# Two-layer encoder trunk on one core: the order of the first FFN's start, the norms behind the mixers, the first mixer's attention gaps and one weight split of the second mixer are changed

## The chip, the cores and the metric

The kernel runs on one NeuronCore of a Trainium2 chip. The metric is device time in microseconds from launch to end; a lower time is better. The core has five engines that run side by side, each through its own list of instructions in order: TensorE (PE, matmuls), VectorE (DVE), ScalarE (ACT), GpSimd (POOL) and SyncE (SP, which only issues transfers). They wait for each other through semaphores.

## The reference

Two groups of tokens (512 and 256, model width 1024) go through the same two layers. Everything is float32.

```python
def swiglu(h, wg, wu, wd):
    return (jax.nn.silu(h @ wg) * (h @ wu)) @ wd          # 1024 -> 2816 -> 1024

def even_layer(x, ...):
    x = x + 0.5 * swiglu(rmsnorm(x, f1_n), f1_g, f1_u, f1_d)
    x = x + mixer_ab(rmsnorm(x, mix_n), ...)   # gated MLP | windowed attention (8 heads, 2 kv heads)
    x = x + 0.5 * swiglu(rmsnorm(x, f2_n), f2_g, f2_u, f2_d)

def odd_layer(x, ...):
    x = x + 0.5 * swiglu(...)
    x = x + mixer_c(rmsnorm(x, mix_n), ...)    # 2-D neighbourhood attention, 16 heads, then @ w_out
    x = x + 0.5 * swiglu(...)

y = rmsnorm(odd_layer(even_layer(x)), final_norm)
```

## The kernel before

The 768 tokens are one block of columns. An activation tile holds 128 features on the partitions and up to 768 tokens; work goes by halves of 384 tokens. A float32 product is made of three passes over halves of the operands: `wsplit` (L113) cuts a weight block of 128x512 into a rounded high part `whi` (cast on ACT, L125) and the rest `wlo` (a subtraction on DVE or POOL, L126). `split` (L221) does the same with activations (names ending in h and l, L224 and L225). A product needs high x high, high x low and low x high.

The six stages are FFN, first mixer, FFN, FFN, second mixer, FFN, with a norm between them. The FFNs take the 2816 hidden columns in 11 pairs of blocks and use seven products per 2x2 step instead of eight. The products are called b11, b21, t2, t3, n4, t1 and b22 in the order of use, each for the gate and then for the up weights; each is 12 matmuls of 384 columns for gate and 12 for up. Weight sums (`s`, L817) and activation sums (`tmp`, L439) feed some of them. The first four pairs are early pairs: their b11 and b21 are computed while the norm of the tokens isn't known yet, so the norm's factors come in later. Four matmuls with a diagonal matrix (`diag`, L326 and L324, against `onesr`) spread the factors of the tokens over the partitions, two for each half of the tokens.

The behaviour that the change touches:

- **Start.** `tok_norm` (L275) squares six token blocks for each half on ACT (L289) and takes the mean's power -0.5 on POOL (`rsqrt`, L337). `rest` (L441) makes the operands t3, n4, t1 and b22 on ACT and DVE. `hidden` (L625) takes gate and up to the gated hidden value: two products with the norm's factors (L631, L633), silu on ACT (L632) and the product sg·v (L634, `scalar_tensor_tensor`). `settle` (L723) runs the last five products of an early pair, and `parts` (L586) makes a weight operand one product ahead.
- **Norm behind a mixer.** `norm_half` (L358) calls `norm_tok` (L256). Without `power`, `rsqrt` computes the reciprocal root on DVE by Newton steps on 128x3 tiles (L341 to L350).
- **First mixer's attention.** `attention` (L1349) is a generator beside the projections. In each of twelve rounds it traces a `score` (L1291), the `values` (L1328) of the round before, and the `turn` (L1315): a transpose of the probabilities `p` by matmuls with the identity (`ident`). The yields between them are delays in modelled PE time, so they set how many projection matmuls stand between; the gap is 5.2 us in the model.
- **Output product of the second mixer.** `mixer_out` (L1050) is used by both mixers; `begun` is set in the first one only. `rows(m)` (L1095) loads and splits the weights of output block m. In the second mixer `ready` (L1066) traces the splits of the attention's output ahead of `rows(0)`. `oh` and `ol` are the halves of the attention's output `o`, six blocks for each half of the tokens.

PE's order is the order of the trace, steered by these delays. The orders of DVE, ACT, POOL and SP are set by a scheduler by priorities; `high_priority` moves work forward, and `issue_after(x)` keeps an instruction behind x. POOL also issues some weight transfers (L108).

Of the kernel before, what the change touches and what calls it, by code (L numbers as in the profile page):

```python
# [9 lines left out]
F32 = mybir.dt.float32  # L10
# [4 lines left out]
ALU = mybir.AluOpType  # L15

P = 128
# [38 lines left out]
class Trunk:  # L56
# [4 lines left out]
    def __init__(self, ctx, tc, aps, phases=PHASES):  # L61
        self.tc, self.nc, self.aps, self.phases = tc, tc.nc, aps, phases
        self.units = []
        self.woff = self.pi = 0
        self.t = 0.0
        self.chains = []
        self.spare = []
        self.first = []
        self.copied = []
        self.ps1 = []  # L70
        self.exps = []
        self.hids = []
        self.tok = []
        pool = lambda name, bufs, **kw: ctx.enter_context(tc.tile_pool(name=name, bufs=bufs, **kw))
        self.cp = pool("const", 1)
        self.xp = pool("x", 1)
        self.rawp = pool("raw", 4)
        self.wp = pool("w", NW)
        self.np_ = pool("norm", 1)
        self.sp = pool("small", 1, side="right")  # L80
        self.mm = pool("mm", 4, space=bass.MemoryType.PSUM)
        self.aux = pool("aux", 4, space=bass.MemoryType.PSUM)
        self.dram = pool("spill", 1, space=bass.MemoryType.DRAM)
        self.guards = {}
        self.side = "left"
# [29 lines left out]
    def wsplit(self, src, eng=None, keep=False):  # L115

        nc = self.nc
        self.pi += 1
        if keep:
            hi, lo = (self.fw.tile([P, 512], F32R, tag="s", name=f"k{n}{self.pi}", bufs=8) for n in ("hi", "lo"))  # L120
        else:
            hi = self.wp.tile([P, 512], F32R, tag="whi", name=f"whi{self.pi}")
            lo = self.wp.tile([P, 512], F32R, tag="wlo", name=f"wlo{self.pi}")
        hi, lo = (t.rearrange("p (a b) -> p a b", a=src.shape[1]) for t in (hi, lo))
        self.cast = nc.scalar.copy(hi, src).ins  # L125
        (eng or nc.gpsimd).tensor_tensor(out=lo, in0=src, in1=hi.bitcast(F32), op=ALU.subtract)  # L126
        return hi, lo

    def unit(self, name, k0, nk, c0, n):
# [145 lines left out]
    def tok_norm(self, h):  # L275

        nc = self.nc
        while len(self.copied) < TOKW[h]:
            yield 0.2
        sm = self.sp.tile([P, 3, 6], F32, tag="sm", name="sm", bufs=3)  # L280
        it = self.sp.tile([P, 6], I32, tag="smi", name="smi", bufs=2)
        a, y, b = (sm[:, i, :3] for i in range(3))
        for i in range(6):
            if h:
                with self.tc.issue_after(self.loading):
                    self.tok_load()
            t = self.tok[6 * h + i]
            with self.tc.issue_after(self.copied[-1]) if h else nullcontext():
                nc.scalar.activation(t, t, AF.Square, accum_out=(b if i % 2 else a)[:, i // 2 : i // 2 + 1])  # L289
        with self.tc.high_priority() if h == 0 else nullcontext():  # L290
            nc.vector.tensor_tensor(out=a, in0=a, in1=b, op=ALU.add)
            self.rsqrt(y, a, 1.0 / D, a, b, it[:, :3], True)
            self.early[h] = self.diags(y)
        self.spawn(self.norm_rt(h, DELAYT[h]))
# [63 lines left out]
    def norm_half(self, h, d0=1.8, d1=4.0):  # L358

        c0, c1 = HALVES[h]  # L360
        yield d0
        if not self.tok:
            with self.tc.high_priority():
                y = self.norm_tok(self.acc, c0, c1)
        yield d1
        with self.tc.high_priority():
            self.r[h] = self.spread(self.early[h]) if self.tok else self.norm_spread(y)
# [73 lines left out]
    def rest(self, *after):  # L441

        (a0, a1), (c0, c1) = HALVES
        yield STEPS[0]
        fresh = bool(self.tok)
        while fresh and (len(self.copied) < 6 or not self.early):
            yield 0.2
        self.holds = [self.copied[5], self.rooted] if fresh else list(after)
        for n in ("t3", "n4", "t1", "b22"):
            while fresh and n == "b22" and len(self.copied) < 2 * EARLY:  # L450
                yield 0.2
            for k in range(4):
                with ExitStack() as stack:
                    for ins in self.holds + ([self.copied[2 * EARLY - 1]] if fresh and n == "b22" else []):
                        stack.enter_context(self.tc.issue_after(ins))
                    if fresh and n == "t3":
                        stack.enter_context(self.tc.high_priority(offset=500))
                    if n == "t1":
                        self.gain_split(n, k, self.tmp[k], k, self.ngains)
                    elif n == "t3":  # L460
                        t = self.etile("tmp")
                        self.combine(t, self.x[k][:, c0:c1], -1, k, self.tmp[k + 4])
                        self.split(*self.b[n][k], t)
                    elif n == "n4":
                        t = self.tmp["t2", k]
                        self.combine(t, self.x[k + 4][:, a0:a1], 0, k + 4, t)
                        self.split(*self.b[n][k], t)
                    else:
                        self.split(*self.b[n][k], self.tmp[k + 4])
                yield STEPS[1]  # L470
            self.made += [n]

# [42 lines left out]
    def ffn(self, pre):  # L515
# [49 lines left out]
        def pair(p):  # L565
# [9 lines left out]
                        a[n, i + 1, 1], a[n, i + 1, 2] = r[:, 0:4, :], r[:, 4:8, :]  # L575

            h = hs[p] = {}
            s, bank, e = {}, {}, {}
            steps = iter(())

            def sums(n, name):
# [4 lines left out]
            def parts(n, b):  # L586
                name = {"t2": "s2", "t3": "s3", "t1": "s1", "b22": "s4"}.get(b)
                soon = fresh and not p and b == "t3"
                with self.tc.high_priority(offset=500 if soon else None) if b == "t2" and p in urgent or soon else nullcontext():
                    return self.wsplit(sums(n, name) if name else a[n, 2, 2], nc.vector)  # L590

            def product(n, w, b, key, start, st=None):
# [29 lines left out]
                nc.vector.tensor_tensor(out=t, in0=bank[key, n], in1=t, op=ALU.add)  # L622
                next(steps, None)

            def hidden(i, half, g, u):  # L625

                self.run_until(lambda: half in scales)
                h[i, half] = t = g if half else etile("sg")
                v = u if half else etile("v")
                r = rt[:, HALVES[half][0] : HALVES[half][1]]  # L630
                nc.vector.tensor_tensor(out=t, in0=g, in1=r, op=ALU.mult)  # L631
                nc.scalar.activation(t, t, AF.Silu, scale=-1.0 if i else 1.0)  # L632
                self.freed = nc.vector.tensor_tensor(out=v, in0=u, in1=r, op=ALU.mult).ins  # L633
                nc.vector.scalar_tensor_tensor(out=t, in0=t, scalar=-0.5 if i else 0.5, in1=v, op0=ALU.mult, op1=ALU.mult)  # L634

            def begin(n, p1):

# [76 lines left out]
            def entry(ahead=False):  # L714
                if not loaded:
                    settled()
                    loaded.append(True)
                if ahead:
                    return None
                with self.tc.issue_after(self.hids[1]) if fresh and not p else nullcontext():  # L720
                    return parts("gate", "t2")

            def settle(st):  # L723

# [2 lines left out]
                for i, (n, b) in enumerate(todo):  # L727
# [14 lines left out]
                    if n == "up":  # L742
                        if b == "t3":
                            fourth()
                        if b == "n4":
                            hidden(1, 0, bank["Y", "gate"], bank["Y", "up"])
                        elif b == "t1":
                            hidden(1, 1, e["gate", "u3"], e["up", "u3"])
                        elif b == "b22":
                            hidden(0, 1, e["gate", "u2"], e["up", "u2"])  # L750

            if early:
# [4 lines left out]
                p2()  # L757
                yield
                with self.tc.high_priority():
                    hidden(0, 0, bank["X", "gate"], bank["X", "up"])  # L760
                self.hids.append(self.freed)
                yield
            if early:
# [6 lines left out]
            if early:  # L770
                if p + 1 < EARLY - 1:
                    addeds[p + 1](behind + 3 if fresh and p == 0 else None)
                settle(now)
            else:
                for f in (p1, p6, p2, p7, p4, p5, p3) if p == NPAIR - 1 else (p1, p6, p2, p7, p5, p3, p4):
                    f()
# [273 lines left out]
    def mixer_out(self, name, ot, chain, cols=False, begun=None):  # L1050
# [44 lines left out]
        def rows(m):  # L1095
# [1 line left out]
                loaded[4] = self.raw(name, 0, 4, m * P, 2 * P)  # L1097
                loaded[2] = self.unit(name, 4, 2, m * P, 2 * P)
            c = m % 2 * P
            hi, lo = self.wsplit(loaded[4][:, :, c : c + P], self.nc.vector if begun and m < 3 else None)  # L1100
            return [(hi[:, k, :], lo[:, k, :]) for k in range(4)] + [tuple(t[:, c : c + P] for t in k) for k in loaded[2]]

        def first(m, h, w):
# [106 lines left out]
    def mixer0(self):  # L1210
# [138 lines left out]
        def attention(gap):  # L1349
            cur = None  # L1350
            for kv in (0, 1):
                for n in range(6):
# [5 lines left out]
                    if cur:  # L1358
                        values(*cur[:3], tt)
                        valued.append(cur[:2])  # L1360
                    yield gap
                    cur = new
                    tt = turn(*cur)
                    yield 0.3 * gap
            yield 1.0
            values(*cur[:3], tt)

# [555 lines left out]
```

## Time and profile before

| | us |
|---|---|
| three runs | 2575.41, 2578.79, 2583.24 |
| median | 2578.79 |
| profiled execution | 2577.02 |
| its span, first to last instruction | 2575.3 |
| PE, DVE, ACT, POOL busy | 2548.0, 2204.1, 1365.4, 225.3 |

The profile is of one execution. A page gives busy times, the span in 40 slices, the chain of work that ended last and the costliest groups. Beside it the trace answers questions on a stretch: a timeline row gives start, duration, engine, line, output<-input, shapes, and in brackets the idle time of the engine ahead of it and what ended it. Matmuls are pipelined, so a matmul's duration overlaps the next one's; distances between their starts are what counts. Where a matmul waits, its pipeline refills too, so that PE loses somewhat more than the idle time in brackets. A row of slices gives the time, PE's busy time and number of matmuls, the granted clock of PE (1.00 is full speed), the DMA engines' share and GB/s.

### The profile page before, as it was taken

The page shows a single profiled execution, that of the slowest core. Times are in us where ns is not written, and L with a number is a line of the kernel's source. Part 1 is how long each engine was busy: PE and PEld are TensorE (multiplying, and loading weights), DVE is VectorE, ACT ScalarE, POOL GpSimd, SP SyncE. Part 2 cuts the span into 40 slices and gives each one's busy share as a digit, 9 for nine tenths or more (in the row PEclk, how much of TensorE's full clock was granted, in tenths as well). Part 3 has the DMA queues.
Part 4 walks back from the last instruction along what each step waited for, and adds up shares of the span by engine and source line. Part 5 has one row for each costly group of instructions (what it writes and reads, how often), then busy time and mean ns, then how long its engine had stood idle before and what let it go on. Part 6 is the DMA issues. An engine that isn't in the chain of part 4 may idle for free.

```text
span 2575.3 us, 41296 instructions
## 1 busy us (share of the span) xinstructions
PE 2548.0 (99%) x15114; PEld 2487.0 (97%) x15114; DVE 2204.1 (86%) x4558; ACT 1365.4 (53%) x2869; POOL 225.3 (9%) x355
## 2 busy tenths in 40 slices
PE   9999999999999999999999999999999999999998
PEld 8999999988899999999999999999899999999997
DVE  7988898888889889889998889986777699888897
ACT  7544454556666545445654445454545475454543
POOL 2100000000031320000100000002222221000000
PEclk9999999999999999999999999999999999999999
DMA  8422221421236432222542222242221354222222
GB/s 266 111 82 66 79 70 66 147 78 54 66 120 159 126 120 69 73 78 81 149 98 82 69 80 66 66 146 64 64 64 41 108 151 103 87 76 68 74 67 74
DMA packets 84029, 238.68 MB, mean 93 GB/s; under 512 B 10481, under 2 KB 19505, under 8 KB 83825
## 3 DMA queue, kind: packets, MB, share of 16 engines
q1 hardware_dynamic: 69136, 204.93, 24.3%
q0 software_dynamic: 14400, 30.81, 6.0%
q8 instruction: 119, 1.95, 0.3%
q14 instruction: 86, 0.70, 0.1%
q10 hardware_dynamic: 288, 0.29, 0.0%
HBM read 226.56 MB, written 15.07 MB: 94 GB/s over the span
## 4 chain that ended last, share of the span: by engine, by line
PE 89%; DVE 7%; ACT 2%; issue 1%; DMA 1%; POOL 0%; SPq 0%; DVEq 0%; ACTq 0%; POOLq 0%
PE ps_mm L155 54%; PE ps_aux L155 33%; DVE wlo L126 1%; PE ps_aux L159 1%; DMA raw<-in_w 1%; ACT p L1195 1%; DVE p L1189 1%; DVE p L1205 0%; DVE tmp L439 0%; DVE tl L225 0%; DMA tok<-in_xt 0%; ACT whi L125 0%; DVE sg L634 0%; DVE s L817 0%; DVE o L1341 0%
## 5 line engine op out<-in xcount | busy, mean ns | idle before, releaser
L125 ACT CAST whi<-s 128x512 fp32r<-128x512 f32 x496 | 304.4, 620 | 398.4 <-DVE s L817 118.1
L125 ACT CAST whi<-raw 128x512 fp32r<-128x512 f32 x472 | 286.8, 618 | 222.5 <-PE ps_mm L155 85.4
L126 DVE TENSOR_TENSOR wlo<-s,whi 128x512 fp32r<-128x512 f32 x496 | 337.4, 686 | 67.6 <-ACT whi L125 61.2
L126 DVE TENSOR_TENSOR wlo<-raw,whi 128x512 fp32r<-128x512 f32 x439 | 300.8, 692 | 19.0 <-ACT whi L125 15.5
L155 PE MATMUL ps_mm<-db,whi 128*128 128x384 f32 x864 | 219.2, 334 | 0.0
L155 PE MATMUL ps_aux<-dt,whi 128*128 128x384 f32 x864 | 219.2, 334 | 0.0
L155 PEld LDWEIGHTS ps_aux<-dt,whi 128*128 128x128 f32 x864 | 156.0, 188 | 0.0
L155 PEld LDWEIGHTS ps_mm<-db,whi 128*128 128x128 f32 x864 | 156.0, 188 | 0.0
L155 PE MATMUL ps_mm<-xh,whi 128*128 128x512 f32 (+1 forms) x416 | 145.0, 349 | 0.0
L155 PE MATMUL ps_aux<-dt,wlo 128*128 128x384 f32 x432 | 144.3, 334 | 0.0
L155 PE MATMUL ps_mm<-db,wlo 128*128 128x384 f32 x432 | 144.3, 334 | 0.0
L155 PE MATMUL ps_mm<-xl,whi 128*128 128x512 f32 (+1 forms) x416 | 140.2, 337 | 0.0
L155 PE MATMUL ps_mm<-xh,wlo 128*128 128x512 f32 (+1 forms) x416 | 140.2, 337 | 0.0
L108 POOL DMA_DIRECT2D s<-in_w x96 | 75.0, 858 | 693.2 <-PE ps_aux L155 306.8
L622 DVE TENSOR_TENSOR u<-ps_aux,u 128x384 f32<-128x384 f32 x176 | 97.2, 552 | 9.5 <-PE ps_aux L155 9.4
L155 PE MATMUL ps_aux<-dh,whi 128*128 128x384 f32 x384 | 97.5, 334 | 0.0
L1195 ACT ACTIVATE p<-p,st 128x256 f32<-128x256 f32 (+3 forms) x144 | 68.9, 480 | 52.8 <-DVE st L1193 52.7
L873 DVE TENSOR_TENSOR x<-ps_aux,x 128x384 f32<-128x384 f32 x160 | 85.1, 552 | 12.0 <-PE ps_aux L155 11.9
L873 DVE TENSOR_TENSOR x<-ps_mm,x 128x384 f32<-128x384 f32 x160 | 86.5, 552 | 5.3 <-PE ps_mm L155 5.0
L155 PEld LDWEIGHTS ps_mm<-xh,whi 128*128 128x128 f32 x416 | 78.9, 190 | 9.0 <-issue 0.7
L155 PEld LDWEIGHTS ps_mm<-xh,wlo 128*128 128x128 f32 x416 | 78.8, 189 | 8.6
L617 ACT COPY u<-ps_mm 128x384 f32<-128x384 f32 x176 | 83.2, 473 | 6.7 <-PE ps_mm L155 6.6
(520 smaller groups left out, 8187.6 us busy)
## 6 DMA issues: line engine op xcount, KB each, us to landing
raw<-in_w SPq DMA_DIRECT2D x282, 512.0 KB, 3.6
s<-in_w POOLq DMA_DIRECT2D x96, 256.0 KB, 4.3
row<-in_w SPq DMA_DIRECT2D x32, 512.0 KB, 3.7
row<-in_w SPq DMA_DIRECT2D x32, 256.0 KB, 3.9
xdm<-x SPq DMA_DIRECT2D x16, 384.0 KB, 2.4
x<-in_x SPq DMA_DIRECT2D x16, 192.0 KB, 4.7
tok<-in_xt SPq DMA_DIRECT2D x12, 256.0 KB, 6.1
xold<-xdm SPq DMA_DIRECT2D x8, 384.0 KB, 3.0
```

The source lines that it names most:

```text
L108: ins = (eng or self.nc.sync).dma_start(raw, src, **kw).ins
L125: self.cast = nc.scalar.copy(hi, src).ins
L126: (eng or nc.gpsimd).tensor_tensor(out=lo, in0=src, in1=hi.bitcast(F32), op=ALU.subtract)
L155: self.nc.tensor.matmul(out, lhsT=lhsT, rhs=rhs, start=start, stop=stop, **kw)
L159: self.nc.tensor.transpose(out, src, self.ident)
L617: nc.scalar.copy(e[n, out], bank[key, n])
L622: nc.vector.tensor_tensor(out=t, in0=bank[key, n], in1=t, op=ALU.add)
L873: nc.vector.tensor_tensor(out=o, in0=ps, in1=o, op=ALU.add)
L1189: nc.vector.tensor_tensor_reduce(out=outs[i], in0=ps_list[i], in1=adds[i], scale=1.0, scalar=init[i], op0=ALU.add, op1=ALU.max, accum_out= ...
L1195: ins = nc.scalar.activation(outs[i], outs[i], AF.Exp, bias=nm[:, i : i + 1], accum_out=sm[:, i : i + 1])
```

## The change

It has five parts. (1) In the first FFN: the token squares of the second half wait for operand t3 and, the last two, for the cast of pair 0's first t2 weights; the loads of their tokens are traced at once; some weight sums are kept behind a first low half (`self.lower`), the b22 sums behind the n4 operands. (2) In early pairs, the product sg·v of two `hidden` calls, (0, 0) and (1, 0), is put off to the end of `settle`, and in pair 0 the whole call (1, 1). (3) `norm_half` passes `self.mixed` as `power`: both mixers' norms take the power on POOL. (4) In `mixer_out` the low half of block 0's weights is made on DVE in the second mixer as well, where before POOL made all of them (L1100); the first mixer's blocks 0 to 2 stay on DVE. (5) In `attention` the delays are 0.8 and 0.5 of the gap instead of 1.0 and 0.3.

```diff
-        (eng or nc.gpsimd).tensor_tensor(out=lo, in0=src, in1=hi.bitcast(F32), op=ALU.subtract)
+        low = (eng or nc.gpsimd).tensor_tensor(out=lo, in0=src, in1=hi.bitcast(F32), op=ALU.subtract).ins
+        if eng is nc.vector and not self.marked:
+            self.lower = low
...
+        for _ in range(6 * h):
+            with self.tc.issue_after(self.loading):
+                self.tok_load()
         for i in range(6):
-            if h:
-                with self.tc.issue_after(self.loading):
-                    self.tok_load()
             t = self.tok[6 * h + i]
-            with self.tc.issue_after(self.copied[-1]) if h else nullcontext():
+            while h and (len(self.thirds) < 3 or i >= 4 and not self.marked):
+                yield 0.2
+            with self.tc.issue_after(self.marked if i >= 4 else self.thirds[2]) if h else nullcontext():
...
-                y = self.norm_tok(self.acc, c0, c1)
+                y = self.norm_tok(self.acc, c0, c1, self.mixed)
...
+                    if fresh and n == "n4":
+                        self.negated = self.halved
+                    elif fresh and n == "t3":
+                        self.thirds.append(self.halved)
...
-                with self.tc.high_priority(offset=500 if soon else None) if b == "t2" and p in urgent or soon else nullcontext():
+                with ExitStack() as stack:
+                    if b == "t2" and p in urgent or soon:
+                        stack.enter_context(self.tc.high_priority(offset=500 if soon else None))
+                    if fresh and not p and b == "b22":
+                        stack.enter_context(self.tc.issue_after(self.negated))
+                    if soon or fresh and not p and (n, b) == ("up", "t2"):
+                        stack.enter_context(self.tc.issue_after(self.lower))
...
                         if b == "n4":
-                            hidden(1, 0, bank["Y", "gate"], bank["Y", "up"])
+                            put_off.append(hidden(1, 0, bank["Y", "gate"], bank["Y", "up"], True))
+                        elif b == "t1" and p:
+                            hidden(1, 1, e["gate", "u3"], e["up", "u3"])
                         elif b == "t1":
-                            hidden(1, 1, e["gate", "u3"], e["up", "u3"])
+                            put_off.append(lambda: hidden(1, 1, e["gate", "u3"], e["up", "u3"]))
...
-                    hidden(0, 0, bank["X", "gate"], bank["X", "up"])
+                    put_off.append(hidden(0, 0, bank["X", "gate"], bank["X", "up"], True))
...
                 settle(now)
+                for f in put_off:
+                    f()
...
-            hi, lo = self.wsplit(loaded[4][:, :, c : c + P], self.nc.vector if begun and m < 3 else None)
+            hi, lo = self.wsplit(loaded[4][:, :, c : c + P], self.nc.vector if m < (3 if begun else 1) else None)
...
-                    yield gap
+                    yield 0.8 * gap
                     cur = new
                     tt = turn(*cur)
-                    yield 0.3 * gap
+                    yield 0.5 * gap
```

The orders of both kernels show what moved. Lines of the changed kernel are some 4 to 30 higher than those of before.

DVE in the start of the first FFN, before, from the weight sum ahead of the t3 operands on (`sg`, `v`: of hidden; `s`: weight sums; `t3xl`: low halves of t3; `wlo`: low halves of weights):

```order
L817 TENSOR_TENSOR s_686<-s_584,row 128x512
L225 TENSOR_TENSOR t31l<-tmp,t31h 128x384
L225 TENSOR_TENSOR t32l<-tmp,t32h 128x384
L631 TENSOR_TENSOR sg<-ps_mm_526,acc 128x384
L817 TENSOR_TENSOR s_700<-s_588,row 128x512
L817 TENSOR_TENSOR s_726<-row 128x512
L126 TENSOR_TENSOR wlo_689<-s_686,whi_688 128x512
L633 TENSOR_TENSOR v<-ps_mm_561,acc 128x384
```

and the same place of the changed kernel:

```order
L647 TENSOR_TENSOR sg<-ps_mm_524,acc 128x384
L229 TENSOR_TENSOR t31l<-tmp,t31h 128x384
L229 TENSOR_TENSOR t32l<-tmp,t32h 128x384
L847 TENSOR_TENSOR s_661<-s_582,row 128x512
L649 TENSOR_TENSOR v<-ps_mm_559,acc 128x384
L445 SCALAR_TENSOR_TENSOR tmp<-x_107,ngains,tmp 128x384
L128 TENSOR_TENSOR wlo_664<-s_661,whi_663 128x512
L445 SCALAR_TENSOR_TENSOR tmp<-x_108,ngains,tmp 128x384
```

The two weight sums s_700 and s_726 no longer stand between the first sum and its `wlo`; the first sum itself stands behind t32l. Later on DVE, at the end of pair 0's products, the changed kernel has this (u: products kept in SBUF, s_948: weight sum for pair 1's t2 of up):

```order
L638 TENSOR_TENSOR u_745<-ps_aux_871,u_745 128x384
L652 SCALAR_TENSOR_TENSOR u_768<-u_768,u_789 128x384
L649 TENSOR_TENSOR u_745<-u_745,acc 128x384
L847 TENSOR_TENSOR s_948<-s_671,row 128x512
L652 SCALAR_TENSOR_TENSOR u_720<-u_720,u_745 128x384
L847 TENSOR_TENSOR s_974<-row 128x512
L128 TENSOR_TENSOR wlo_951<-s_948,whi_950 128x512
```

where before the like sum s_951 stood ahead of the add u_749 that waits for PE:

```order
L225 TENSOR_TENSOR b223l<-tmp,b223h 128x384
L817 TENSOR_TENSOR s_922<-s_692,row 128x512
L622 TENSOR_TENSOR u_724<-ps_aux_852,u_724 128x384
L817 TENSOR_TENSOR s_951<-s_696,row 128x512
L126 TENSOR_TENSOR wlo_925<-s_922,whi_924 128x512
L631 TENSOR_TENSOR u_724<-u_724,acc 128x384
L622 TENSOR_TENSOR u_749<-ps_aux_876,u_749 128x384
```

PE in the first mixer, third round, before (turn: `ident,p`; projection: `xh`, `xl`; the next score: `kh,q`):

```order
L159 MATMUL ps_aux_6331<-ident,p 128x128 x4
L155 MATMUL ps_mm_6353<-xh_5221,whi_6269 128x256
L155 MATMUL ps_mm_6353<-xl_5229,whi_6269 128x256
L155 MATMUL ps_mm_6353<-xh_5221,wlo_6270 128x256
L155 MATMUL ps_aux_6357<-kh_5635,q_5916 128x384
```

and changed:

```order
L163 MATMUL ps_aux_6325<-ident,p 128x128 x4
L159 MATMUL ps_mm_6288<-xh_5227,whi_6284 128x512
L159 MATMUL ps_mm_6288<-xl_5235,whi_6284 128x512
L159 MATMUL ps_mm_6288<-xh_5227,wlo_6285 128x512
L159 MATMUL ps_mm_6288<-xh_5228,whi_6284 128x512
L159 MATMUL ps_mm_6288<-xl_5236,whi_6284 128x512
L159 MATMUL ps_mm_6288<-xh_5228,wlo_6285 128x512
L159 MATMUL ps_aux_6343<-kh_5635,q_5916 128x384
```

Three matmuls of 256 columns between turn and score became six of 512. DVE at the output product of the second mixer, changed (`ol`: low halves of the attention's output; wlo_22821: low half of output block 0's weights, which before was POOL's):

```order
L229 TENSOR_TENSOR ol_22770<-o_20333,oh_22762 128x384
L229 TENSOR_TENSOR ol_22771<-o_20901,oh_22763 128x384
L229 TENSOR_TENSOR ol_22772<-o_21251,oh_22764 128x384
L229 TENSOR_TENSOR ol_22773<-o_21828,oh_22765 128x384
L128 TENSOR_TENSOR wlo_22821<-raw_22812,whi_22820 128x512
L128 TENSOR_TENSOR wlo_23008<-raw_23005,whi_23007 128x512
L1598 TENSOR_TENSOR o_22122<-ps_aux_22827,tb 64x512
```

and PE there, in the same order before and after:

```order
L159 MATMUL ps_mm_22716<-xh_18837,wlo_22480 128x256
L159 MATMUL ps_mm_22824<-oh_22760,whi_22820 128x384
L159 MATMUL ps_mm_22824<-oh_22760,wlo_22821 128x384
L159 MATMUL ps_aux_22827<-th,vt 128x2x128
```

The low half that PE's third row needs stands behind all twelve `ol` of DVE in the changed kernel.

More of the change, by code (lines that the diff above doesn't have):

```diff
@@ L66, in __init__ @@
         self.chains = []
+        self.marked = None
+        self.thirds = []
         self.spare = []
@@ L577, in pair @@
             h = hs[p] = {}
-            s, bank, e = {}, {}, {}
+            s, bank, e, put_off = {}, {}, {}, []
             steps = iter(())
@@ L623, in add, with hidden @@
                 next(steps, None)
-            def hidden(i, half, g, u):
+            def hidden(i, half, g, u, later=False):
                 self.run_until(lambda: half in scales)
@@ L633, in hidden, with gated @@
                 self.freed = nc.vector.tensor_tensor(out=v, in0=u, in1=r, op=ALU.mult).ins
-                nc.vector.scalar_tensor_tensor(out=t, in0=t, scalar=-0.5 if i else 0.5, in1=v, op0=ALU.mult, op1=ALU.mult)
+                def gated():
+                    nc.vector.scalar_tensor_tensor(
+                        out=t, in0=t, scalar=-0.5 if i else 0.5, in1=v, op0=ALU.mult, op1=ALU.mult
+                    )
+                if later:
+                    return gated
+                gated()
             def begin(n, p1):
@@ L720, in entry @@
                 with self.tc.issue_after(self.hids[1]) if fresh and not p else nullcontext():
-                    return parts("gate", "t2")
+                    st = parts("gate", "t2")
+                self.marked = self.cast
+                return st
             def settle(st):
```

## Prediction

> **What bounds the kernel now.** I read the page's busy table and its chain, then the list of what TensorE (PE) waited for, then single stretches of the timeline where one of those waits lies.
>
> ```profile
> PE 2548.0 (99%) x15114; PEld 2487.0 (97%) x15114; DVE 2204.1 (86%) x4558; ACT 1365.4 (53%) x2869; POOL 225.3 (9%) x355
> PE 89%; DVE 7%; ACT 2%; issue 1%; DMA 1%; POOL 0%; SPq 0%; DVEq 0%; ACTq 0%; POOLq 0%
> PE ps_mm L155 <- DVE wlo L126: 3.1, 3, 2.0
> PE ps_aux L155 <- DVE tl L225: 2.9, 7, 0.8
> PE ps_aux L155 <- DVE b223l L225: 1.4, 1, 1.4
> PE ps_mm L155 <- POOL wlo L126: 0.5, 1, 0.5
> ```
>
> PE is busy 99% of 2575.3 us, and 89% of the chain is PE. The change takes no matmul away and adds none, so it can win only PE's waits and half-speed stretches, and it loses by new ones. The waits are few, and each stands at one place. The sum below is therefore a list of places, made against the profiled execution's 2577.0 us. The median of the three runs, 2578.8, is 1.8 above it; a difference within 0.3% (7.7 us) is what a measurement here cannot tell from no change.
>
> **1. The start (gain).** The first rows are slices of 3.4 us: PE busy, then the granted clock. The rest are timeline rows of PE, ACT and DVE.
>
> ```profile
> 42.04:45.46 3.42, 1.25 (x6) 1.00 1.04 372
> 45.46:48.87 3.41, 1.97 (x6) 0.50 0.26 104
> 48.87:52.28 3.41, 3.41 (x12) 0.50 1.02 223
> 59.10:62.50 3.40, 2.06 (x9) 1.00 1.06 322
> 62.50:65.90 3.40, 3.40 (x12) 0.50 0.36 114
> 43.56 0.61 ACT L125 CAST whi<-s 128x512 fp32r<-128x512 f32 x1
> 46.90 0.69 PE L155 MATMUL ps_mm<-t20h,wlo 128*128 128x384 f32 x1 [2.05 <-DVE wlo L126]
> 53.30 0.34 PE L155 MATMUL ps_mm<-t30h,whi 128*128 128x384 f32 x1
> 57.47 0.33 PE L155 MATMUL ps_mm<-n40h,whi 128*128 128x384 f32 x1
> 60.09 0.44 PE L155 MATMUL ps_mm<-n42h,whi 128*128 128x384 f32 x1 [1.07 <-ACT n42h L224]
> 62.13 0.34 PE L155 MATMUL ps_mm<-n40h,whi 128*128 128x384 f32 x1
> 50.63 1.96 DVE L634 SCALAR_TENSOR_TENSOR sg<-sg,v 128x384 f32<-128x384 f32 x4
> 84.40 0.33 PE L155 MATMUL ps_mm<-n40h,whi 128*128 128x384 f32 x1
> ```
>
> A product is 24 matmuls; t3 takes 57.47 − 53.30 = 4.17 us at full clock, 0.174 a matmul. Before, wlo stands third behind two sums of weights (L817), and half of the token squares stand on ACT ahead of the casts. In the new order the sums and squares of later use go behind. Replaying the new orders by hand with the durations above, whi ends at 44.8, wlo at 45.8 (before 46.9). The clock comes back one slice earlier, since 45.46 to 48.87 is then nearly all work: t2 (24 matmuls) ends at 51.05, before at 53.30: **−2.25**. The n4 gate (57.47 to 62.13) takes 4.66 us where its 12 matmuls need 2.08; with n40 and n41 cast earlier and the two diag matmuls moved behind it, I find a wait of 0.6, so 2.7: **−1.9**. With that, the half clock of 62.50 to 65.90 goes: twelve matmuls in 3.4 us become 2.08, **−1.3**, less 0.37 for the two diag matmuls, plus as much at the slice's edges. The wait for b223l, 1.4 and its fill, goes, since its cast now stands far ahead and four products sg·v (0.47 each) move behind it: **−1.55**.
>
> What is late next: pair 1's weight sum s (DVE row 107 of the new order) stands behind u for b22's up half, which waits for PE. From b22's end three DVE rows at 0.47, the sum at 0.6, the cast at 0.55 and one more sum with wlo at 1.2 stand in line: 2.8 us to whi and 4.0 to wlo. PE has 12 matmuls, 2.08 us, to do meanwhile: a new wait of 0.75 for whi and 0.75 for wlo, up to 2.2 where ACT's silu gets ahead of the cast. I take **+1.7** (so pair 1's n40h at 84.40 − 7.0 + 1.7 = 79.1) and +0.5 for a half slice that it may bring (idle 2.17 of 3.42 brought one, above, and 1.34 of 3.40 too). Sum **−4.8**, bounds −6.5 (no new wait) and −2 (the second half slice stays).
>
> The same deferral of sg·v in the other 15 early pairs moves two or three rows of 0.47 behind the next operands. PE waits at hardly one of these places (the list of waits above has three for wlo in all), so I cost it at nothing; without cover it is 0.5 a place.
>
> The Trainium skill's page "TensorE: Matmul & The Clock Gate", § What's actually happening, has the clock halve after a whole idle window of about 3.4 us. The rows speak against it: two windows that were 36% and 61% busy were each followed by a half-clock one. By its rule the −1.3 would not exist and the new wait could bring no half slice: −4.0 instead of −4.8.
>
> **2. Norms behind both mixers (gain).** Thirteen tiny DVE operations give way to one on DVE and one on POOL, at four places.
>
> ```profile
> 789.86 0.15 DVE L349 TENSOR_TENSOR sm<-sm 128x3 f32<-128x3 f32 x1
> 53.42 1.11 POOL L337 TENSOR_TENSOR sm<-sm,space 128x3 f32<-128x3 f32 x1 [4.24 <-DVE sm L336]
> 53.18 0.61 DVE L439 SCALAR_TENSOR_TENSOR tmp<-x,ngains,tmp 128x384 f32<-128x384 f32 x1
> 789.93 0.61 DVE L431 SCALAR_TENSOR_TENSOR t11l<-tmp,ngains,t11h 128x384 fp32r<-128x384 f32 x1
> 791.13 0.68 DVE L126 TENSOR_TENSOR wlo<-s,whi 128x512 fp32r<-128x512 f32 x1
> 791.87 0.44 PE L155 MATMUL ps_mm<-t30h,wlo 128*128 128x384 f32 x1 [0.53 <-DVE wlo L126]
> 792.67 0.88 PE L155 MATMUL ps_aux<-diag,onesr 128*128 128x384 f32 x2
> ```
>
> A tiny operation starts 0.07 behind the one ahead of it (789.86 to 789.93), so 13 are 0.9 us of DVE; the deferred sg·v take another 2 us from ahead of it. PE's wait at 791.87 (0.7 with its fill) and the one at 792.67 (0.37) close, and their like in the second layer: **−2.0**. DVE's yh must now wait for POOL, 1.11 us: if nothing stands between, that gives back 0.3 to 0.8 a place. On POOL the power stands between weight DMAs (L108), which then go out about 1.1 us later; their sums stand several DVE rows behind, so this costs nothing unless those rows run dry. Bounds −2.5 and 0.
>
> "SBUF — State Buffer", § Who interferes with whom (the Trainium skill), has a DVE operation with two SBUF inputs and a GpSimd one that reads SBUF shut each other out. By that the power could hold DVE 1 us at four places, a sum of +2 instead of −2. Row 53.18, with two SBUF inputs, has its 0.61 us beside the power of 53.42, so here I don't count it.
>
> **3. First mixer (gain).** The scores come farther behind the turn, the turn nearer behind the values.
>
> ```profile
> L155 PE MATMUL ps_aux<-kh,q 64*128 64x256 f32 (+1 forms) x96 | 16.5, 334 | 2.8 <-DVE tl L225 1.8 <-DVE o L1416 0.7 <-DVE q L1471 0.2
> 632.40 0.38 PE L155 MATMUL ps_aux<-kh,q 64*128 64x256 f32 x1
> 634.37 0.39 PE L155 MATMUL ps_mm<-xh,whi 128*128 128x256 f32 x1
> 573.01 0.44 PE L155 MATMUL ps_aux<-kh,q 64*128 64x384 f32 x1
> 583.96 1.39 DVE L1205 TENSOR_SCALAR p<-p,st 128x384 f32<-128x384 f32 x4
> 586.13 1.56 PE L159 MATMUL ps_aux<-ident,p 128*128 128x128 f32 x12
> 647.11 0.44 PE L155 MATMUL ps_aux<-kh,q 64*128 64x384 f32 x2
> 654.79 1.07 DVE L1205 TENSOR_SCALAR p<-p,st 128x384 f32<-128x384 f32 x3
> 659.37 1.48 PE L159 MATMUL ps_aux<-ident,p 128*128 128x128 f32 x12
> ```
>
> A score of 12 matmuls needs a psum bank that DVE frees late. At 632.40 it takes 1.97 us, though the eleven behind the wait need 0.90: 1.0 lost. The row of all 96 shows 2.8 idle, of which 0.7 is this place: with the same share of refill (1.0 for 0.7) they lose 4 to 5.5. With 0.35 to 1.4 us more products ahead of each score, 4.5 of that go. Against it: the turn needs p. Of the score of 573.01 the p are ready at 585.35, 0.8 ahead of the turn; of that of 647.11 at 655.9, 3.5 ahead. The new order has 0.3 to 1.5 us less work between a score and its turn, so three or four of twelve would wait, 0.5 each: +2.0. **−2.5**, bounds −5 and +1.
>
> **4. Second mixer's output (loss).** The low half of the first output block's weights moves from POOL to DVE.
>
> ```profile
> 1989.06 1.28 POOL L126 TENSOR_TENSOR wlo<-raw,whi 128x512 fp32r<-128x512 f32 x1 [3.08 <-ACT whi L125]
> 1989.67 1.56 DVE L225 TENSOR_TENSOR ol<-o,oh 128x384 fp32r<-128x384 f32 x2
> 1990.39 0.44 PE L155 MATMUL ps_mm<-oh,wlo 128*128 128x384 f32 x1 [0.50 <-POOL wlo L126]
> 1992.95 4.30 DVE L225 TENSOR_TENSOR ol<-o,oh 128x384 fp32r<-128x384 f32 x9
> 1997.17 0.67 DVE L1568 TENSOR_TENSOR o<-ps_aux,tb 64x512 f32<-64x512 f32 x1
> ```
>
> POOL had it ready at 1990.34 and PE waited 0.5. In the new order it is a DVE operation behind all twelve ol, while PE's second matmul of the block still needs it. These rows and the short ones between them fill DVE from 1989.67 to 1997.17, with no idle time in front of any. Less 0.54, since beside POOL one ol took 1.1 and not 0.55, wlo starts at 1996.6, ends at 1997.3, and PE goes on at 1997.4 instead of 1990.4: **+7.0**. Queued behind it on PE are the turns and values that DVE and ACT wait for next, so nothing else proceeds. Seven idle us hold a whole slice of 3.4, so the clock halves: between half of one slice and of 1.5, 0.9 to 2.6, I take **+1.7**. Sum **+8.7**, bounds 0 (PE would have other rows ahead of it, which the order denies) and +10.
>
> **Sum:** 2577.0 − 4.8 − 2.0 − 2.5 + 8.7 = 2576.4; with the runs' median a little above the profiled one, **2577**.
>
> **Rivals.** *The ol wait does not hold (faster).* If the low half got out ahead of the second six ol, whose casts ACT ends late, the loss would be 2 to 3, or 0. For it: ACT and DVE pace those splits. Against: an engine keeps its order, and the rows below 1988 are full. Without the term: 2577 − 8.7 = **2568**.
>
> *The turns wait for p (slower).* The p of 573.01 come 12.3 us behind their score's first matmul, those of 647.11 8.8; the turns stand 13.1 and 12.3 behind, and some 11 in the new order. From a mean lag of 11 on, every one of the twelve turns waits, 1 us a time with its refill: instead of −2.5 it is +12 − 4.5 = +7.5, and 2576.4 + 10 = **2586**. For it: DVE is the busiest engine after PE (86%), and its splits come earlier there. Against: 12.3 holds a delay of the score itself, and 8.8 has room.
>
> *The change does not do what it says.* If every gain came to a third (start −1.6, norms −0.7, mixer −0.8), with the loss as above, it is +5.6: **2583**, within the bound; its share is in the middle.
>
> **How the numbers follow.** The sum with its terms' bounds (2571 to 2585) 0.68; the wait does not hold, 0.18; turns wait, 0.14. So faster by over 0.3% 0.18, the same 0.68, slower 0.14. The range reaches to the other cases: 2567 to 2586.
>
> **What would show it.** Step 1: pair 1's n40h at about 79 instead of 84.40, one half-clock slice instead of three before 66 us, and a wait of 1.5 for DVE's wlo at 70 to 73. Step 2: no wait for wlo near 790. Step 3: the kh,q idle of 2.8 falls below 1, and a PE wait for p (0.3 in the list of waits) rises to 1 to 2.5. Step 4: one PE wait for wlo of 6 to 7 us near 1980, with slices at clock 0.5 behind it. If that one is missing, the forecast falls.

## Result and profile after the change

The changed kernel takes 2590.52 us (median of 6 runs, 2587.53 to 2592.78) beside 2577.98 for before (6 runs): ratio 1.0049, interval 1.0039 to 1.0059. It is 12.5 us slower, and it lies outside the range of the prediction. The profiled execution took 2591.38 us.

The page's span and busy table, then lines of PE's list of waits for the changed kernel (us in total, times, longest; line numbers are its own: L128 is the weights' low half, L163 the turn, L228 and L229 the activation halves, L633 the copy `keep`, L652 sg·v):

```profile
span 2589.5 us, 41249 instructions
PE 2550.3 (98%) x15114; PEld 2489.7 (96%) x15114; DVE 2197.5 (85%) x4511; ACT 1365.6 (53%) x2869; POOL 228.1 (9%) x358
PE ps_mm L159 <- DVE wlo L128: 8.0, 3, 7.5
PE ps_mm L159 <- ACT oh L228: 4.9, 1, 4.9
PE ps_mm L159 <- ACT whi L127: 3.3, 2, 2.2
PE ps_aux L163 <- DVE o L1371: 2.2, 2, 1.3
PE ps_mm L159 <- DVE sg L647: 1.9, 2, 1.1
PE ps_mm L159 <- ACT u L633: 1.6, 1, 1.6
PE ps_aux L163 <- DVE p L1235: 0.3, 1, 0.3
```

PE's busy time hardly moved (2548.0 before); the span grew by waiting. Three waits in the list are large and new: 7.5 us for one low half, 4.9 for `oh`, and 2.2 for `o` ahead of turns.

To place all of the loss, I took the distance from each matmul's start to the next one's and subtracted 0.4515 ns for each of its columns (0.1734 us for 384 columns, the spacing at full clock), but at least 0.064 us, a flat allowance for the shortest matmuls that is the same in every row. What is left is PE time that isn't matmul, idle, refill and half clock alike, in us by stretches of the span:

| kernel | 0–75 | 75–505 | 505–740 (first mixer) | 740–1700 | 1700–2060 (second mixer) | 2060–end | all |
|---|---|---|---|---|---|---|---|
| before | 18.4 | 0.4 | 12.6 | 4.3 | 15.8 | 5.8 | 57.2 |
| changed | 13.0 | 3.0 | 21.7 | 3.3 | 25.3 | 5.2 | 71.5 |
| e1_pool_row0 | 12.8 | 2.2 | 20.9 | 4.2 | 15.8 | 5.2 | 61.2 |
| e2_old_gaps | 11.9 | 2.1 | 12.5 | 3.3 | 24.6 | 4.4 | 58.8 |
| e3_round11 | 12.6 | 2.3 | 14.7 | 2.1 | 24.5 | 4.3 | 60.6 |
| e4_both_back | 12.8 | 2.6 | 12.5 | 2.7 | 15.6 | 3.5 | 49.8 |

The first two rows differ by 14.3, which is all of the 14.4 between the two profiled executions. The start gained 5.4 and lost 2.6 again behind it; the second mixer lost 9.5, near the forecast; the first mixer lost 9.1 where I had forecast a gain.

**The start.** Slices of 3.4 us with PE busy and the granted clock, and two timeline rows of PE in the changed kernel:

```profile
42.04:45.46 3.42, 1.25 (x7) 1.00 0.92 349
45.46:48.87 3.41, 3.16 (x10) 0.53 0.44 160
48.87:52.28 3.41, 3.41 (x21) 0.97 0.67 170
72.00 0.44 PE L159 MATMUL ps_mm<-t20h,whi 128*128 128x384 f32 x1 [1.14 <-ACT whi L127]
78.80 0.33 PE L159 MATMUL ps_mm<-n40h,whi 128*128 128x384 f32 x1
```

One slice is at half clock instead of three, and pair 1's n40h starts at 78.80 (before 84.40; I had worked out 79.1). The new wait at pair 1's t2 is there, too. It brought no half clock: the slice around it (69.30 to 72.70 us, PE busy 2.18 of 3.40) was followed by one at 1.00.

**The first mixer's output product.** Timeline rows of PE, then of ACT, around the 4.9 us wait:

```profile
673.19 0.47 PE L159 MATMUL ps_aux<-kh,q 64*128 64x256 f32 x2
675.15 0.34 PE L159 MATMUL ps_mm<-eh,wlo 128*128 128x384 f32 x1
680.38 0.58 PE L159 MATMUL ps_mm<-oh,whi 128*128 128x384 f32 x1 [4.89 <-ACT oh L228]
680.76 0.52 PE L159 MATMUL ps_mm<-oh,wlo 128*128 128x384 f32 x1
681.08 0.52 PE L159 MATMUL ps_mm<-oh,whi 128*128 128x384 f32 x1
681.40 0.52 PE L159 MATMUL ps_mm<-oh,wlo 128*128 128x384 f32 x1
676.45 1.28 ACT L1225 ACT_TABLE_LOAD   x1
677.75 0.51 ACT L1225 ACTIVATE p<-p,st 128x256 f32<-128x256 f32 x1
679.73 0.19 ACT L1230 ACTIVATE st<-st 128x4 f32<-128x4 f32 x1
679.82 1.74 ACT L228 CAST oh<-o 128x384 fp32r<-128x384 f32 x4
```

ACT does a table load and the exponentials of a whole attention round, 3.4 us, and only then the four casts of `oh` that PE's next matmul needs. Behind the wait the matmuls start 0.32 apart instead of 0.17: the clock is halved. Before the change, the last six casts stood ahead of the same table load:

```profile
675.70 2.60 ACT L224 CAST oh<-o 128x384 fp32r<-128x384 f32 x6
678.31 1.28 ACT L1195 ACT_TABLE_LOAD   x1
```

**The second mixer's output product.** PE, DVE, and the slices behind:

```profile
1994.81 0.44 PE L159 MATMUL ps_mm<-oh,whi 128*128 128x384 f32 x1
2002.79 0.69 PE L159 MATMUL ps_mm<-oh,wlo 128*128 128x384 f32 x1 [7.54 <-DVE wlo L128]
1997.84 4.30 DVE L229 TENSOR_TENSOR ol<-o,oh 128x384 fp32r<-128x384 f32 x9
2002.05 1.28 DVE L128 TENSOR_TENSOR wlo<-raw,whi 128x512 fp32r<-128x512 f32 x2
2001.30:2004.70 3.40, 1.91 (x7) 0.50 0.99 349
2004.70:2008.10 3.40, 3.40 (x14) 0.50 0.99 362
```

The low half comes right behind the last of the twelve `ol`, as the order said.

### The profile page after: what moved, and what is told of

It is laid out like the page before. It is cut to its first block, busy times and chain, and to the rows that moved or that the text cites. A ratio compares the mean times of both kernels' runs of the same rounds, so it can differ in the third digit from the quotient of the medians.

```text
span 2589.5 us, 41249 instructions
## 1 busy us (share of the span) xinstructions
PE 2550.3 (98%) x15114; PEld 2489.7 (96%) x15114; DVE 2197.5 (85%) x4511; ACT 1365.6 (53%) x2869; POOL 228.1 (9%) x358
## 4 chain that ended last, share of the span: by engine, by line
PE 89%; DVE 7%; ACT 2%; DMA 1%; issue 1%; POOL 0%; DVEq 0%; ACTq 0%; POOLq 0%
PE ps_mm L159 54%; PE ps_aux L159 33%; DMA raw<-in_w 1%; DVE wlo L128 1%; PE ps_aux L163 1%; ACT p L1225 1%; DVE p L1219 0%; DVE p L1235 0%; DVE s L847 0%; DVE tl L229 0%; ACT whi L127 0%; DVE dt L229 0%; DVE ol L229 0%; DVE u L638 0%; DVE acc L255 0%
## 5 line engine op out<-in xcount | busy, mean ns | idle before, releaser
L128 DVE TENSOR_TENSOR wlo<-s,whi 128x512 fp32r<-128x512 f32 x496 | 336.7, 684 | 68.9 <-ACT whi L127 61.9
L128 DVE TENSOR_TENSOR wlo<-raw,whi 128x512 fp32r<-128x512 f32 x440 | 301.4, 691 | 19.4 <-ACT whi L127 15.7
L1225 ACT ACTIVATE p<-p,st 128x256 f32<-128x256 f32 (+3 forms) x144 | 69.0, 480 | 62.1 <-DVE st L1223 62.0
L159 PE MATMUL ps_mm<-oh,wlo 128*128 128x384 f32 x252 | 86.2, 342 | 7.5 <-DVE wlo L128 7.5
L159 PE MATMUL ps_mm<-oh,whi 128*128 128x384 f32 x252 | 87.7, 348 | 4.9 <-ACT oh L228 4.9
```

The source lines that it names most:

```text
L128: low = (eng or nc.gpsimd).tensor_tensor(out=lo, in0=src, in1=hi.bitcast(F32), op=ALU.subtract).ins
L159: self.nc.tensor.matmul(out, lhsT=lhsT, rhs=rhs, start=start, stop=stop, **kw)
L1225: ins = nc.scalar.activation(outs[i], outs[i], AF.Exp, bias=nm[:, i : i + 1], accum_out=sm[:, i : i + 1])
```

## Experiments

Each is the changed kernel with the edit shown. Times are medians beside runs of the kernel before on the same chip.

**Row 0's low half back on POOL.**

```diff
-            hi, lo = self.wsplit(..., self.nc.vector if m < (3 if begun else 1) else None)
+            hi, lo = self.wsplit(..., self.nc.vector if begun and m < 3 else None)
```

> The changed kernel, with the low half of output block 0's weights in the second mixer made on POOL again. Theory A (the low half behind the twelve ol costs 8.9 us: PE's wait of 7.5 and the half clock behind it): 2590.5 - 8.9 = 2581.6, the 7.5 us wait for DVE's wlo is gone and one of 0.5 for POOL's is back. Rival B (the seven idle us let DVE and ACT run ahead, so that other waits of the second mixer come back once it is gone): 2586 or more, and waits of 3 us or more appear between 1700 and 2060 us.

2579.71 us, ratio to before 1.0007 (0.9998 to 1.0017). Against the changed kernel it is 10.8 less; the second mixer's stretch is at 15.8 again, as before the change, and no wait came in its place. Its wait there, from the list between 1960 and 2020 us:

```profile
PE ps_mm L159 <- POOL wlo L128: 0.5, 1, 0.5
```

Theory A holds, rival B doesn't.

**The old delays in the first mixer.**

```diff
-                    yield 0.8 * gap
+                    yield gap
...
-                    yield 0.5 * gap
+                    yield 0.3 * gap
```

> The changed kernel with the first mixer's old delays (1.0 and 0.3 of the gap). Theory A (the new delays cost 8.6 us in the first mixer, most of it PE's wait of 4.9 us for the oh casts at 675 us): 2582, no wait for oh above 0.3, the kh,q idle is back at 2.8. Rival B (that wait comes from the start's shift or the norms and not from the delays): 2589 to 2591 with the wait for oh still there.

2578.44 us, ratio 1.0006 (0.9996 to 1.0015): 12.1 less than the changed kernel, more than expected. The first mixer's stretch is at 12.5, the wait for `oh` is gone and the waits of before are back. So the new delays are the cause; 9.2 of the 12.1 are in that stretch, and I can't place the rest better than as small differences in all the others.

**The output's casts one round earlier.** `exps` holds the last exponential of each attention round traced so far. The first mixer's output product keeps its casts behind the last entry. The expectation calls the two rounds the eleventh and the twelfth. By the traces they are the ninth and the tenth of the twelve: before the change the casts start at 667.8 us, right behind the last row of the ninth softmax (667.7), and the four late casts of the changed kernel at 679.82, right behind that of the tenth (679.73).

```diff
-            with self.tc.high_priority(), self.tc.issue_after(self.exps[-1]):
+            with self.tc.high_priority(), self.tc.issue_after(self.exps[-2]):
                 parts(rest, 0)
```

> The changed kernel with the new delays, but the splits of the attention's output in the first mixer's output product are kept behind the eleventh round's exponentials and not behind the last ones traced, which with the new delays are the twelfth round's. Theory A (the last score is now traced ahead of that place, so the four oh casts stand behind the twelfth softmax on ACT): the wait of 4.9 for oh falls below 0.5 and the half clock at 680 goes, 2590.5 - 6.5 = 2584. Rival B (ACT is simply late there: the casts wait for DVE's o): 2589 to 2591, PE waits as long for oh or ol.

2582.31 us, ratio 1.0018 (1.0008 to 1.0027): 8.2 less than the changed kernel. The orders of PE, POOL and SP are the same in both; on ACT the `oh` casts moved from behind to ahead of the tenth round's exponentials, and on DVE the `ol` and a few rows behind them followed. The end of the difference on ACT (L1225 and L1230 are the tenth round's softmax):

```
 L1225 ACTIVATE p,st<-p,st 128x256 x4
 L1230 ACTIVATE st<-st 128x4
-L228 CAST oh_7502<-o_5838 128x384
-L228 CAST oh_7503<-o_5839 128x384
-L228 CAST oh_7504<-o_5840 128x384
-L228 CAST oh_7505<-o_5841 128x384
```

PE's first `oh` matmul and the ACT rows behind the casts:

```profile
673.93 0.33 PE L159 MATMUL ps_mm<-eh,wlo 128*128 128x384 f32 x1
674.10 0.33 PE L159 MATMUL ps_mm<-oh,whi 128*128 128x384 f32 x1
672.24 1.76 ACT L228 CAST oh<-o 128x384 fp32r<-128x384 f32 x4
675.70 1.28 ACT L1225 ACT_TABLE_LOAD   x1
```

There is no gap at all between the two matmuls. That settles the mechanism: the changed delays let the attention run ahead in the trace, its tenth score is now traced ahead of the output product's casts, and a condition that took the ninth round takes the tenth.

**Both taken back.** The edits of the first and second experiment together:

```diff
+            hi, lo = self.wsplit(..., self.nc.vector if begun and m < 3 else None)
...
+                    yield gap
...
+                    yield 0.3 * gap
```

> The changed kernel without these two parts: row 0's low half on POOL and the old delays; the start's order, the deferred products and the norms by power are left. Theory A (the two losses are separate places and add): 2590.5 - 8.9 - 8.6 = 2573.0, that is 5 us less than before: about 2.6 from the start and early pairs, the rest from norms and first mixer. Rival B (only the two places together explain it, the rest gained nothing): 2577 to 2578.

2569.85 us, ratio 0.9973 (0.9961 to 0.9984): faster than before by 0.27%. The two losses add within the noise (10.8 and 12.1 alone, 20.7 together, each uncertain by some 2.5). What is left of the change gains 7.4 in the table: 5.6 in the start, 3.9 between 740 us and the end without the second mixer, less 2.2 between 75 and 505.

**Mended casts with the new delays, and POOL.** The edits of the first and third experiment:

```diff
+            hi, lo = self.wsplit(..., self.nc.vector if begun and m < 3 else None)
...
+            with self.tc.high_priority(), self.tc.issue_after(self.exps[-2]):
```

> Row 0's low half on POOL and the output's splits of the first mixer behind the eleventh round, with the change's delays (0.8 and 0.5). Theory A (with the oh wait mended, the new delays still cost: the turn's wait of 2.2 for DVE's o outweighs the score waits that they save): first mixer 14.7 instead of the old delays' 12.5, so 2569.85 + 2.2 = 2572. Rival B (the delays gain once the casts are in place, as I had forecast): 2567.4.

2573.67 us, ratio 0.9989 (0.9980 to 0.9998). In its first mixer PE waits

```profile
PE ps_aux L163 <- DVE o L1371: 2.2, 2, 1.3
PE ps_aux L159 <- DVE tl L229: 1.6, 4, 0.8
PE ps_aux L163 <- DVE p L1235: 1.0, 1, 1.0
```

and that stretch loses 16.3, with the old delays 12.5. Theory A: apart from the accident at the output, the delays don't gain, and by this stretch they cost 3.8; the two times differ by as much (2573.67 and 2569.85), though their intervals overlap a little. The waits ahead of scores fell only from 2.8 to 1.8 (a wait of 0.4 for `o` ahead of another product went, too), and turns now wait for `o`, DVE's additions that take the round's values out of psum (the memory that matmuls write to), and once for p.

**Turn as before, scores farther.** The kernel just above, with one edit more:

```diff
-                    yield 0.8 * gap
+                    yield gap
```

> Row 0's low half on POOL, the output's splits of the first mixer behind the eleventh round, the turn at 1.0 of the gap behind the values as before and the scores at 0.5 behind the turn as in the change. Theory A (the nearer turn waits for DVE's o of the values, 2.2 us; the farther scores do save their bank wait): the first mixer loses 10 instead of 12.5 of the base, 2569.85 - 2.5 = 2567.4. Rival B (longer rounds push the last rounds behind the projections, where nothing covers them): 2570 to 2575.

2580.86 us, ratio 1.0014 (1.0005 to 1.0024): a miss, of rival B's kind but worse than its 2575. The rounds are longer, the last turn starts only at 719.6 us with no projection between it and the values around it, and the first mixer's stretch loses 23.4. Its longest waits:

```profile
PE ps_aux L159 <- DVE tl L229: 3.6, 8, 1.3
PE ps_aux L159 <- DVE vhl L229: 1.7, 1, 1.7
PE ps_mm L159 <- DVE rt L1276: 0.9, 1, 0.9
```

**Row 0 on DVE, but written ahead.** The base is the kernel with both taken back.

```diff
+            hi, lo = self.wsplit(..., self.nc.vector if m < (3 if begun else 1) else None)
...
-            w = []
+            w = [rows(0)]
             with self.tc.high_priority():
                 parts(early[:2], 0)
```

> The base (2569.85) with row 0's low half in the second mixer on DVE, but with its load and split written ahead of the output's splits, so that it stands behind two ol and two qk and not behind twelve ol. Theory A (the place in DVE's order costs, not the engine): PE's wait there is 0.5 to 1.3, 2570.3. Rival B (DVE is too late with anything there, or the load is): the wait stays at 3 to 7, 2573 to 2578.

2572.65 us, ratio 0.9978 (0.9968 to 0.9989). The low half stands behind two `ol` and two `qk`, and PE waits 2.1 for it. That is more than theory A's 0.5 to 1.3 and less than rival B's 3 to 7. DVE's rows there:

```profile
1985.40 1.02 DVE L229 TENSOR_TENSOR ol<-o,oh 128x384 fp32r<-128x384 f32 x2
1986.34 0.75 DVE L1704 TENSOR_TENSOR qk<-ps_mm,rt 128x256 f32<-128x256 f32 x2
1987.01 0.68 DVE L128 TENSOR_TENSOR wlo<-raw,whi 128x512 fp32r<-128x512 f32 x1
```

The place sets the size of the wait, 7.5 or 2.1 on the same engine. But POOL, which is free there, still has it earlier (0.5).

**No power on POOL.** The kernel with both taken back, and the norms behind the mixers as before the change:

```diff
-                y = self.norm_tok(self.acc, c0, c1, self.mixed)
+                y = self.norm_tok(self.acc, c0, c1)
```

> The run before with both losses taken back (2569.85), and now the norms behind both mixers by Newton steps on DVE again instead of the power on POOL. Theory A (the freed DVE time closes the waits at the norms): +2.0, 2571.9, with the 0.5 us waits for wlo near 790 and 2110 back. Rival B (the deferred sg.v alone freed DVE there, the power is hidden anyway): 2569.9 within 0.7.

2571.14 us, ratio 0.9969 (0.9959 to 0.9978), that of its base 0.9973 (0.9961 to 0.9984): the times don't tell them apart. The traces' sums differ by 1.8 (51.6 and 49.8), 1.5 of it between 2060 and 2300 us. A gain is not shown. And theory A's sign failed: the 0.5 us waits for wlo near 790 and 2110 did not come back. All that the list has of DVE's wlo is

```profile
PE ps_mm L159 <- DVE wlo L128: 0.2, 1, 0.2
```

**Deferral in pair 0 alone.** The kernel with both taken back, and sg·v done at once in pairs 1 to 3 of each FFN. The edit stands at both calls that defer this product only; one is shown:

```diff
-                    put_off.append(hidden(0, 0, bank["X", "gate"], bank["X", "up"], True))
+                    put_off.append(hidden(0, 0, bank["X", "gate"], bank["X", "up"], not p) or (lambda: None))
```

> The same base (2569.85) with the product sg.v deferred in pair 0 only and done at once in pairs 1 to 3. Theory A (the deferred products hold their operand tile, so ACT's copy of u waits for DVE's sg and PE for that copy, 1.6 us near 101 us): that wait goes, 2569.85 - 2 = 2568. Rival B (the copy waits because DVE is late as a whole): the wait stays or moves by less than 0.5 us, and waits near 790 grow: 2570 to 2571.

2572.60 us, ratio 0.9980 (0.9970 to 0.9989). PE's wait for ACT's copy of u falls from 1.6 to 0.2, as theory A said, but 1.9 come back before 75 us and 1.8 behind 2060. The sum is no gain, where theory A had 2 us.

**Deferral in all early pairs but pair 1.** The same place:

```diff
+                    put_off.append(hidden(0, 0, bank["X", "gate"], bank["X", "up"], p != 1) or (lambda: None))
```

> Both losses taken back as in the base (2569.85), with the products sg.v done at once in pair 1 and deferred in pairs 0, 2 and 3. Theory A (pair 1's deferral holds the tile that ACT's copy of u waits for, 1.6 us near 101 us, and the other pairs' deferral is what keeps the waits at pairs 2 and 3 small): 2569.85 - 1.8 = 2568. Rival B (pair 1's products at once put DVE behind in the start, as the deferral in pair 0 alone did, 1.9 us before 75 us): 2570 to 2572.

2569.22 us, ratio 0.9974 (0.9965 to 0.9983). The stretch from 75 to 505 us loses 0.1 instead of 2.6; the whole comes to 49.0 in place of 49.8. So pair 1's deferral makes the wait at 101 us, and what it saves elsewhere is nearly as large. By its times this version equals the one with both taken back; both beat the two kernels of this case.

## Why the prediction was wrong

The sum was −4.8 −2.0 −2.5 +8.7. In the traces the four steps came to about −2.8, −1.6, **+9.1** and +9.5.

**Step 3, the first mixer, is the step that failed.** It held that the delays change only the distances inside a round: waits ahead of scores go (−4.5) and turns wait for p (+2.0). I followed PE's order between turn and score, but not the place where the attention's tenth round passes the point at which the output product is written. The row that says it was in the new order of ACT, four `oh` casts behind that round's softmax. It costs 4.9 us of wait, the refill and a half-clock slice, 7.0 together in the table (21.7 to 14.7), where the sum had nothing. The two terms that I did list were wrong as well: the turns wait for `o` (2.2 us at two places), which I had not named, and for p no more than before (0.3). The score waits gave back 1.0 of idle and not the larger part of 2.8:

```profile
L159 PE MATMUL ps_aux<-kh,q 64*128 64x256 f32 (+1 forms) x96 | 15.8, 330 | 1.8 <-DVE tl L229 1.6 <-DVE q L1501 0.2
```

As far as the list shows, these waits are what is left of the loss, 2.1 in the table; no run takes the waits for `o` out by themselves. The rival that came nearest in time, turns that wait for p, has the wrong mechanism: no run shows more than 1.2 of that wait.

**Step 1 was right in mechanism, mis-sized by one term.** Up to pair 1's n4 the parts came about as worked out: one half-clock slice, the b223l wait gone, a new wait of 1.1 to 1.3 for pair 1's t2, 78.80 for 79.1; the half slice that the new wait might bring (+0.5) did not come. The term costed at nothing, the deferral in the other early pairs, cost 2.6. DVE's late sg·v holds a tile of a rotating set (`etile`), ACT's copy waits for that tile, and PE waits for the copy:

```profile
102.36 0.55 DVE L652 SCALAR_TENSOR_TENSOR sg<-sg,v 128x384 f32<-128x384 f32 x1
102.94 0.48 ACT L633 COPY u<-ps_mm 128x384 f32<-128x384 f32 x1 [0.62 <-DVE sg L652]
103.48 0.44 PE L159 MATMUL ps_mm<-n40h,whi 128*128 128x384 f32 x1 [1.63 <-ACT u L633]
```

I had counted what the deferred operation does, 0.47 us later, and not what its operands keep from others. The experiments on pairs 0 and 1 show the link.

**Step 2** came out near its size (−1.6 from 740 us on without the second mixer), but its mechanism isn't shown. The waits for wlo near 791 and 2113 are gone, and they stay gone in the run without the power, and in the one that defers in pair 0 alone; so no run shows which part closed them. Two waits of 0.8 and 1.1 for sg ahead of b11 stand near 774 and 2104 in the changed kernel; with both losses taken back they are gone. How much is the power's and how much the deferral's stays open. The other price weighed there, a power that holds DVE for a microsecond, doesn't show: a weight sum that began while POOL was at the power took its usual 0.68 us, here and again at 2118.37:

```profile
788.18 0.88 POOL L343 TENSOR_TENSOR sm<-sm,space 128x3 f32<-128x3 f32 x1 [9.08 <-DVE sm L342]
788.48 0.68 DVE L847 TENSOR_TENSOR s<-s,row 128x512 f32<-128x512 f32 x1
```

**Step 4** held. Wait 7.5 for 7.0, half clock and refill 2.0 for 1.7; taking it back gave 10.8 in the times and 9.5 in the stretch. The rival that denied this wait falls.

The start again has a half-clock slice behind one that was 37% busy (1.25 of 3.42 us). The Trainium skill's rule of a whole idle window ("TensorE: Matmul & The Clock Gate", § What's actually happening), weighed in step 1, doesn't agree with that row, and the row decides.

## What to carry to other kernels

A condition such as "behind the last one so far" takes its meaning from the trace's order. When delays between generators change, list each place that asks for the latest of something, and see which one it now gets. When an operation is deferred, price the buffers that it holds, not its duration. And compare the new order on every engine that feeds the bound one, at the seams between stages above all.

## What the runs showed of the hardware

The clock halved behind stretches that weren't idle throughout: 45.46 to 48.87 us at 0.53 behind a slice with PE busy 1.25 of 3.42 us. Behind a slice with PE busy 2.18 of 3.40 us (69.30 to 72.70) it stayed at 1.00. It was still at 0.50 for a slice that was busy throughout (2004.70 to 2008.10), behind one that was busy 1.91 of 3.40 us. The return to the exponentials costs ACT 1.28 us of table load, so a cast that slips behind a softmax waits for more than the softmax.
